# A macaron decoder layer on one core: the gate-and-up sevens read a bank on VectorE and store from GpSimd, and loads, norms and an SSD merge are re-timed

## The chip, the cores and the metric

The kernel runs on one core of a Trainium2 chip. It is written by hand against the engines: TensorE (PE) multiplies, VectorE (DVE), ScalarE (ACT) and GpSimd (POOL) do the elementwise work, SyncE (SP) issues most of the transfers, and ACT and POOL issue some. The metric is the device time of one execution in microseconds; of several executions the median is taken. The median before is 2687.21 us (three runs, 2687.17 to 2689.84).

## The reference

One decoder layer on 1024 tokens of width 1024, all in float32:

```python
f = swiglu(rmsnorm(h, ffn1_pre_g), ffn1_w_gu, ffn1_w_down)
h = h + 0.5 * rmsnorm(f, ffn1_post_g)
m = hybrid_mixer(rmsnorm(h, mix_pre_g), ...)   # stick-breaking attention | Mamba-2 SSD, then w_out
h = h + rmsnorm(m, mix_post_g)
c = memory_cross_attention(rmsnorm(h, xa_pre_g), rmsnorm(mem, mem_g), xa_wq, xa_wkv, xa_wo)
h = h + rmsnorm(c, xa_post_g)
f = swiglu(rmsnorm(h, ffn2_pre_g), ffn2_w_gu, ffn2_w_down)
h = h + 0.5 * rmsnorm(f, ffn2_post_g)
```

with `swiglu(h, w_gu, w_down) = (silu(g) * u) @ w_down`, where `g` and `u` are the halves of `h @ w_gu`, and a hidden width of 2816. `rmsnorm` divides by the root of the mean square over the width and multiplies by a gain.

## The kernel before

**Precision.** Each float32 operand is split into a high and a low part (`split`, L262: the high part is a ScalarE cast, L263, the low part a VectorE subtraction, L265). A product takes three matmuls of 128x512: high x high, low x high, high x low (`mm3`). Names that end in `hi`/`h` and `lo`/`l` are such parts; `wraw`, `raw`, `oraw` are tiles as they were loaded.

**Stages.** In the order of time: ffn1's up half (to 457 us), its down half (`down_first`, to about 640), the mixer's SSD projections and scan (`ssd`, about 740 to 1040), attention (to about 1600), the mixer's output (`mix_out`, to about 1750), cross-attention (`xattn`, to about 2040), ffn2's up half (to about 2490) and its down half.

**The sevens.** The up half of each ffn computes gate and up for pairs of feature blocks by a scheme that needs seven products for eight. One call of `seven` (L751) makes a pair `f`: seven products of twelve matmuls each into PSUM banks (`a`, `b`, `c`, `m6`), and between them VectorE, ScalarE and GpSimd add and subtract what the banks hold. There are 38 sevens, 19 in each ffn. The first product goes to `t5` and the second to `d` by ScalarE copies (L758, L762); GpSimd takes `d - t5` (L763, the name `sq` in the profile); VectorE adds the third product to make `e` (L768), and so on; L782 writes the result `t0` (`ft`), L786 and L788 are the last readers of the banks, L789 on GpSimd makes the other result `t1`. Both results are stored to DRAM (`act`) by `store`, which puts the transfer on ScalarE's queue (L622), some 4500 ns of the planner's clock later. The `ft` tiles rotate over NFT buffers, three in ffn1 and four in ffn2. The operands of the seven products are sums and differences of weight blocks, made by GpSimd (L706, `wc`) ahead of time and then split.

**The down half of ffn1** works the same way over units of `act` and `w_dn`; its weight sums (`wsum`, L946 through `add`) start while the last seven still runs.

**What sets the order.** The program order of TensorE is fixed by `_pe` (L100): each matmul is made to follow the one before, and `self.clock` adds an assumed cost of each. Work that is due at a clock time lies in `self.later` and is emitted by `run_later`; `pinned` ties a block to a clock time; `merge` (L156) interleaves two generators in proportion to two given times. For the other engines a scheduler orders the instructions by data and priority; `urgent` (L96) raises the priority. Every engine then runs its own list in order: an instruction that waits holds all behind it.

**Norms.** `post` (L395) books the steps of a post-norm: `cols` (`rms_cols`, L317: TensorE sums `acc` over partitions, `small` in the profile's name, then a root on ScalarE and a reciprocal on VectorE), `rows` (`rms_rows`, L341: a diagonal `dg` on VectorE, L347, and a product with ones), eight `apply` steps, and the columns and rows of the next pre-norm. `times` holds the clock offsets of the first three, `step` the distance of the applies, `tail` the offsets of the pre-norm's two. `sumsq` (L362) squares on ScalarE and adds on VectorE (L370), with a last addition L372 into `acc`. `flush` empties the list and takes over the next norm.

**SSD start.** `bc` (L1360 and after) makes two small products into a `seg` bank, of which there are two; VectorE's L1366 and ScalarE's L1367 empty it.

**Mixer output.** `load` (L1985) loads a piece `oraw`, squares it on ScalarE (L1979 for the first, L1982), and makes `ohi`/`olo` or `xh`/`slo` (`scaled_split`, ScalarE L270 and VectorE L272).

## Time and profile before

| | us |
|---|---|
| median of three runs | 2687.21 |
| profiled execution | 2692.84 |
| its span, first to last instruction | 2691.1 |
| before the first matmul, after the last | 6.9, 7.4 |
| mean granted TensorE clock | 0.987 |

The span is 1.7 us less than the profiled execution's own time, and that execution is 5.6 us longer than the median of the runs. In the rows of the profile a line number is that of the source before; a row names the engine, the line, the operation and output <- inputs; "[x <-y]" at its end says that the engine stood idle for x us just before and what ended that. In the windows each engine's number is its busy time, and the number in brackets the instructions that began.

### The profile page before, as it was taken

What the parts mean: (1) busy time and instruction counts of PE and PEld (TensorE: products, weight loads), DVE (VectorE), ACT (ScalarE), POOL (GpSimd) and SP (SyncE); (2) the same over time, 40 slices, a digit from 0 to 9 for tenths busy, and PEclk for the clock granted to TensorE, in tenths of its full rate; (3) what the DMA queues carried; (4) which work ended last, traced back from release to release, by engine and by line L of the source; (5) the groups of instructions that cost most, each with busy time, mean ns of one, the idle gap of its engine ahead of it and who ended that gap; (6) DMA issues with size and microseconds to landing.
All of it is one profiled execution on the core that took longest, in us unless ns stands there. A gap on an engine that the chain in (4) does not pass through costs nothing. (4 is left out here: it accounts for less than half of the span.)

```text
span 2691.1 us, 36606 instructions
## 1 busy us (share of the span) xinstructions
PE 2602.1 (97%) x12712; PEld 2149.9 (80%) x12712; DVE 1978.3 (74%) x3003; ACT 1272.9 (47%) x2317; POOL 575.7 (21%) x660
## 2 busy tenths in 40 slices
PE   8999999998999999999999999999999999999998
PEld 7788887887777778888888787778777787878887
DVE  7888886888678774777777876674447888876675
ACT  7544443545357783445444553254345443343442
POOL 1655652001100000000000001121112655553000
PEclk9999999998999999999999999999999999999999
DMA  5689887764711225434333468687567455555976
GB/s 207 236 280 316 293 287 242 250 200 152 257 66 47 71 68 188 118 96 113 110 103 107 152 200 315 223 286 248 195 221 269 161 177 193 189 191 196 353 265 219
DMA packets 229593, 528.87 MB, mean 197 GB/s; under 512 B 27936, under 2 KB 37024, under 8 KB 229408
## 3 DMA queue, kind: packets, MB, share of 16 engines
q1 hardware_dynamic: 192352, 419.56, 47.3%
q0 software_dynamic: 24384, 83.90, 8.6%
q10 hardware_dynamic: 12672, 23.07, 2.3%
q8 instruction: 100, 1.64, 0.2%
q14 instruction: 85, 0.70, 0.1%
HBM read 353.41 MB, written 152.04 MB: 188 GB/s over the span
## 5 line engine op out<-in xcount | busy, mean ns | idle before, releaser
L138 PE MATMUL mm<-xh,whi 128*128 128x512 f32 x1288 | 512.3, 407 | 11.4 <-ACT xh L270 6.9
L138 PE MATMUL mm<-xh,wlo 128*128 128x512 f32 x1240 | 479.5, 394 | 0.0
L138 PE MATMUL mm<-xl,whi 128*128 128x512 f32 (+1 forms) x1220 | 477.9, 392 | 0.9 <-DVE xl L265 0.6
L138 PEld LDWEIGHTS mm<-xh,whi 128*128 128x128 f32 x1288 | 244.2, 190 | 55.7 <-ACT xh L270 6.9
L138 PEld LDWEIGHTS mm<-xh,wlo 128*128 128x128 f32 x1240 | 234.4, 189 | 52.3 <-issue 1.3
L138 PEld LDWEIGHTS mm<-xl,whi 128*128 128x128 f32 x1220 | 231.3, 190 | 34.7 <-DVE xl L265 1.4
L1789 DVE TENSOR_TENSOR_SCAN nb<-nb,begin 128x128 f32<-128x128 f32 (+7 forms) x128 | 171.7, 1352 | 57.4 <-ACT nb L1785 56.9
L1785 ACT ACTIVATE nb<-z,scale 128x128 f32<-128x128 f32 (+2 forms) x192 | 108.0, 581 | 88.6 <-PE z L138 87.4
L1822 POOL MEMSET ath<- 128x128 f32 x64 | 13.1, 205 | 496.5 <-PE mm L138 496.5
L263 ACT CAST whi<-wraw 128x1024 fp32r<-128x1024 f32 (+1 forms) x89 | 81.1, 911 | 68.6 <-PE mm L138 37.5
L626 ACT ACTIVATE ft<-ft 128x512 f32<-128x512 f32 x88 | 55.4, 631 | 109.7 <-DVE ft L625 102.2
L706 POOL TENSOR_TENSOR wc<-wraw,raw 128x512 f32<-128x512 f32 x58 | 89.9, 1551 | 70.4 <-DVE whi L265 22.9
L138 PE MATMUL dn<-xh,wlo 128*128 128x512 f32 x296 | 102.1, 393 | 1.7 <-ACT sq L758 1.7
L706 POOL TENSOR_TENSOR wc<-raw,wraw 128x512 f32<-128x512 f32 x56 | 87.3, 1558 | 67.6 <-DVE wlo L265 20.3
L265 DVE TENSOR_TENSOR wlo<-wraw,whi 128x1024 fp32r<-128x1024 f32 x61 | 74.5, 1221 | 34.2 <-ACT whi L263 33.8
L789 POOL TENSOR_TENSOR ft<-ft,e 128x512 f32<-128x512 f32 x38 | 61.9, 1628 | 133.9 <-DVE e L788 66.8
L370 DVE TENSOR_TENSOR acc<-acc,sq 128x512 f32<-128x512 f32 x84 | 56.4, 686 | 46.3 <-ACT sq L369 42.0
L138 PE MATMUL dn<-xh,blk 128*128 128x512 f32 x280 | 90.3, 389 | 0.0
L263 ACT CAST ath<-tr 128x512 fp32r<-128x512 f32 (+1 forms) x108 | 58.9, 547 | 64.5 <-PE tr L141 62.2
L138 PE MATMUL dn<-xh,whi 128*128 128x512 f32 x256 | 88.7, 392 | 0.0
L138 PE MATMUL mm<-ath,v 128*128 128x256 f32 x320 | 85.9, 291 | 2.1 <-DVE sq L1962 2.1
L265 DVE TENSOR_TENSOR atl<-tr,ath 128x512 fp32r<-128x512 f32 (+1 forms) x108 | 67.9, 631 | 24.1 <-ACT ath L263 24.0
(558 smaller groups left out, 6775.6 us busy)
## 6 DMA issues: line engine op xcount, KB each, us to landing
whi<-dwhi SPq DMA_DIRECT2D x57, 512.0 KB, 3.4
wlo<-dwlo SPq DMA_DIRECT2D x57, 512.0 KB, 4.2
wraw<-act SPq DMA_DIRECT2D x102, 256.0 KB, 4.4
raw<-act SPq DMA_DIRECT2D x96, 256.0 KB, 4.5
wraw<-in_w_gu SPq DMA_DIRECT2D x44, 512.0 KB, 4.0
act<-ft ACTq DMA_DIRECT2D x88, 256.0 KB, 2.6
raw<-in_w_gu SPq DMA_DIRECT2D x38, 512.0 KB, 4.4
khi<-whi POOLq DMA_DIRECT2D x30, 512.0 KB, 4.6
```

Source lines behind the costliest of these rows:

```text
L138: self._pe(self.nc.tensor.matmul(out, lhsT, rhs, start=start, stop=stop, skip_group_check=self.more), cost)
L263: self.kp(self.nc.scalar.copy(hi, src))
L265: (eng or self.nc.vector).tensor_tensor(out=lo, in0=src, in1=hi.bitcast(F32), op=ALU.subtract)
L370: self.kp(nc.vector.tensor_tensor(out=accs[i % 2], in0=accs[i % 2], in1=sq, op=ALU.add))
L626: nc.scalar.activation(t, t, AF.Silu)
L706: nc.gpsimd.tensor_tensor(out=t, in0=a, in1=b, op=op)
L789: nc.gpsimd.tensor_tensor(out=t1, in0=t1, in1=e, op=ALU.mult)
L1785: nc.scalar.activation(nb[:, s0:s1], z[:, 0:n], AF.Sigmoid, scale=sc[:, i : i + 1])
L1789: nc.vector.tensor_tensor_scan(out=nb[:, 0:Wd][:, ::-1], data0=nb[:, 0:Wd][:, ::-1], data1=begin[:, S - Wd : S][:, ::-1], initial=0.0, op0 ...
L1822: nc.gpsimd.memset(x[:, 0, :].bitcast(F32), 0.0)
```

## The change

It has nine parts.

1. In `seven`, the second product is no longer copied to SBUF by ScalarE and reduced by GpSimd: VectorE subtracts `t5` from the bank into `d` (new L770).
2. `t1` is stored by a GpSimd transfer right after GpSimd's product that makes it (new L798), instead of by ScalarE later.
3. In ffn2's first block (`f == PLAIN and not begin`), three of the seven sums are made by GpSimd before the first `yield`, into tiles `ts` and `tc` (new L708).
4. In `down_first`, the weight sums of all units but the first two are ordered behind the last reader of the last seven's bank (`self.emptied`).
5. In `down_first`, the squares are urgent, and the clock offsets of both post-norms change.
6. `bc`'s two readers are urgent, and the two given times of the merge at the SSD start change from 3800 against 12110 to 4330 against 9072.
7. `oraw` gets eight buffers instead of four.
8. The mixer's post-norms get `tail` offsets of their own, (18000, 0) and (22000, 0) instead of the default; in `xattn` the steps booked up to `self.posted` are emitted at s == 2, and the rest is flushed at s == 3 instead of 2.
9. Cross-attention's post-norm gets times (8000, 15500, 18500) instead of (7000, 12000, 15000).

```diff
@@ -457,6 +457,7 @@
             c2 = self.t(self.rp, [P, 4], F32, f"cpre{hh}", bufs=2)
             r2_ = self.t(self.rp, [P, H], F32, f"rpre{hh}", bufs=1) if spread else None
             t1, t2 = tail or (t1 + 4000, t2 + 4000)
+            self.posted = T0 + t + 900
             q.append((t + t1, lambda: self.rms_cols([accs2], c2)))
             if spread:
                 q.append((t + t2, lambda: self.rms_rows(c2[:, :], r2_)))
@@ -695,12 +696,19 @@
         def pieces(f):
 
             G, U = (load(wgu[2 * f + i], [P, KT, P]) for i in range(2))
-            yield
             G0, G1, U0, U1 = G[:, 0:4], G[:, 4:8], U[:, 0:4], U[:, 4:8]
-            for a, b, op in (
+            work = [
                 (G0, G1, ALU.add), (U1, None, None), (G0, U1, ALU.add), (U0, G0, ALU.subtract), (G0, None, None),
                 (G1, U1, ALU.subtract), (U0, U1, ALU.add),
-            ):
+            ]
+            if f == PLAIN and not begin:
+                for n, tag, bufs in ((0, "ts", 1), (2, "tc", 2), (3, "tc", 2)):
+                    a, b, op = work[n]
+                    t = self.t(sp2, [P, 4, P], F32, tag, bufs=bufs)
+                    nc.gpsimd.tensor_tensor(out=t, in0=a, in1=b, op=op)
+                    work[n] = t, None, None
+            yield
+            for a, b, op in work:
                 if b is not None:
                     t = self.t(sp, [P, 4, P], F32, "wc", bufs=NWC)
                     nc.gpsimd.tensor_tensor(out=t, in0=a, in1=b, op=op)
@@ -759,8 +767,7 @@
             b = bank()
             product(b, B21)
             with self.urgent():
-                nc.scalar.copy(d, b)
-            nc.gpsimd.tensor_tensor(out=d, in0=d, in1=t5, op=ALU.subtract)
+                nc.vector.tensor_tensor(out=d, in0=b, in1=t5, op=ALU.subtract)
             c = bank()
             product(c, S[1])
             e = es.pop() if es else self.t(sp, [P, H], F32, "e")
@@ -785,10 +792,10 @@
             with self.urgent():
                 nc.vector.tensor_tensor(out=t0, in0=t0, in1=b, op=ALU.mult)
             with self.urgent():
-                nc.vector.tensor_tensor(out=e, in0=e, in1=b, op=ALU.subtract)
+                self.emptied = nc.vector.tensor_tensor(out=e, in0=e, in1=b, op=ALU.subtract).ins
             nc.gpsimd.tensor_tensor(out=t1, in0=t1, in1=e, op=ALU.mult)
             store(f, 0, t0)
-            store(f, 1, t1)
+            nc.gpsimd.dma_start(out=act_d[f // 2][1][:, f % 2, :], in_=t1)
 
         self.nblk = -1
         Wb = blocks()
@@ -943,7 +950,7 @@
             return x[:, 0], x[:, 1]
 
         def add(o, x, y, op):
-            nc.vector.tensor_tensor(out=o, in0=x, in1=y, op=op)
+            return nc.vector.tensor_tensor(out=o, in0=x, in1=y, op=op)
 
         def taker(operands, ahead):
             order = [(p, b) for p in (1, 5, 2, 6, 3, 7, 4) for b in range(NFF // 2)]
@@ -997,7 +1004,9 @@
                 nc.sync.dma_start(out=d, in_=w(0, 1))
                 o = parts(tile, x), parts(place(), y)
                 t = wsum[b] = held(spots[b])
-                add(t, d, y, ALU.subtract)
+                i = add(t, d, y, ALU.subtract)
+                if b > 1:
+                    self._after(i.ins, self.emptied)
                 return o
             if p == 5:
                 x, y = load(a(1, 0), a(1, 1))
@@ -1050,8 +1059,9 @@
         accs = [self.new_accs(), None]
 
         def squares(hh, dh, i0):
-            for i in four:
-                self.sumsq(accs[hh], i0 + i, F[hh][dh][i])
+            with self.urgent():
+                for i in four:
+                    self.sumsq(accs[hh], i0 + i, F[hh][dh][i])
 
         pair = [banks(1), banks(0)]
         product(pair[0])
@@ -1078,7 +1088,7 @@
         squares(0, 1, 4)
         self.norm_pool = self.dnp, 4
         self.XH = [[self.t(self.xp, [P, H], F32R, f"xh{hh}{d}") for d in range(KT)] for hh in range(2)]
-        self.post(0, gpost, self.C[0], gnext, step=4700, accs=accs[0], times=(5000, 8500, 11000), tail=(4500, 8000))
+        self.post(0, gpost, self.C[0], gnext, step=4300, accs=accs[0], times=(8000, 11500, 13500), tail=(4200, 7700))
         ps = banks(0)
         product(ps)
         self.norm_pool = self.msp, 1
@@ -1100,7 +1110,7 @@
             update(F[1][0][i], F[1][0][i], ps[i], ALU.subtract)
             self.sumsq(accs[1], 4 + i, F[1][0][i])
         self.flush(0)
-        self.post(1, gpost, self.C[1], gnext, step=2400, accs=accs[1], times=(4000, 7500, 9500), tail=(15500, 21000))
+        self.post(1, gpost, self.C[1], gnext, step=2400, accs=accs[1], times=(4500, 9500, 11500), tail=(13500, 19000))
 
     def down_seven(self, sp, rw, wdn, act_d, sums_d, out):
 
@@ -1363,8 +1373,9 @@
                 ps = self.t(pp, [P, 2, P], F32, "seg", bufs=2)
                 self.mm(ps[:, 0, :], Bt[:, cs], Ct[:, cs], True, True)
                 self.tr(ps[:, 1, :], Bt[:, cs])
-                nc.vector.tensor_tensor(out=cbm[:, c, :], in0=ps[:, 0, :], in1=self.tri, op=ALU.mult)
-                nc.scalar.copy(Bl[:, c, :], ps[:, 1, :])
+                with self.urgent():
+                    nc.vector.tensor_tensor(out=cbm[:, c, :], in0=ps[:, 0, :], in1=self.tri, op=ALU.mult)
+                    nc.scalar.copy(Bl[:, c, :], ps[:, 1, :])
 
             def early(qd, c):
                 hs = slice(4 * qd, 4 * qd + 4)
@@ -1608,7 +1619,7 @@
 
             for _ in range(6):
                 next(fill)
-            self.merge(first(), 3800, fill_some(fill, 14), 1730 * 14 / 2)
+            self.merge(first(), 4330, fill_some(fill, 14), 648 * 14)
             self.merge(chunks(), 86500, fill, 144000)
             gates()
             self.run_all(keys(6, 8))
@@ -1983,7 +1994,7 @@
                     nc.vector.tensor_tensor(out=asum[-1], in0=asum[-1], in1=sq, op=ALU.add)
 
             def load(kt, hh):
-                raw = self.t(sp, [P, H], F32, "oraw", bufs=4)
+                raw = self.t(sp, [P, H], F32, "oraw", bufs=8)
                 nc.sync.dma_start(out=raw, in_=self.mix_d[kt][:, hh * H : (hh + 1) * H])
                 if kt < 8:
                     square(kt, raw)
@@ -2045,11 +2056,11 @@
                     R.update({i: norm_row(i, 1, 500 + 1000 * i) for i in range(2)})
                 if n == 1:
                     self.run_later(float("inf"))
-                    self.post(0, "mix_post_g", None, "xa_pre_g", step=5000, spread=False)
+                    self.post(0, "mix_post_g", None, "xa_pre_g", step=5000, spread=False, tail=(18000, 0))
                     self.resid(1, 5000, 17000)
                 if n == 3:
                     self.flush(0)
-                    self.post(1, "mix_post_g", None, "xa_pre_g", step=3000, spread=False)
+                    self.post(1, "mix_post_g", None, "xa_pre_g", step=3000, spread=False, tail=(22000, 0))
 
 
     def xattn(self):
@@ -2173,12 +2184,14 @@
                         self.run_all(out_part(ps, next(W), 0, 0, 8))
                         out_copy(ps, 0)
                     self.run_later(float("inf"))
-                    self.post(0, "xa_post_g", None, "ffn2_pre_g", step=5000)
+                    self.post(0, "xa_post_g", None, "ffn2_pre_g", step=5000, times=(8000, 15500, 18500))
                 if s + 2 < 8:
                     load(K, s + 2, "k", 2, 0)
                 if s == 6:
                     self.resid(1, 4000)
                 if s == 2:
+                    self.run_later(self.posted)
+                if s == 3:
                     self.flush(1)
                 if s < 7:
                     step = zip_(values(s), scores(s + 1))
```

How the order on the engines moves, at three places.

GpSimd, around the ends of the first two sevens in ffn1 (`wc` are weight sums, `ft<-ft,e` the product that makes `t1`, `sq<-sq,sq` the subtraction into `d`). Before:

```order
L706 TENSOR_TENSOR wc_1244<-raw_302_1023,wraw_1021 128x512
L789 TENSOR_TENSOR ft_1053<-ft_1053,e_181 128x512
L706 TENSOR_TENSOR wc_1292<-wraw_1021,raw_302_1023 128x512
L763 TENSOR_TENSOR sq_311_1099<-sq_311_1099,sq_310_1098 128x512
L706 TENSOR_TENSOR wc_1322<-raw_302_1023 128x512
L706 TENSOR_TENSOR wc_1350<-raw_328_1173 128x512
L706 TENSOR_TENSOR wc_1399<-raw_328_1173,wraw_1175 128x512
L706 TENSOR_TENSOR wc_1428<-wraw_1175,raw_328_1173 128x512
L789 TENSOR_TENSOR ft_1211<-ft_1211,e_1165 128x512
L706 TENSOR_TENSOR wc_1476<-raw_328_1173,wraw_1175 128x512
L763 TENSOR_TENSOR sq_347_1273<-sq_347_1273,sq_346_1272 128x512
```

The same place in the change, where line numbers above 700 are 7 to 13 higher:

```order
L714 TENSOR_TENSOR wc_1242<-raw_302_1022,wraw_1020 128x512
L796 TENSOR_TENSOR ft_1052<-ft_1052,e_181 128x512
L798 DMA act_45_155<-ft_1052 128x512
L714 TENSOR_TENSOR wc_1291<-wraw_1020,raw_302_1022 128x512
L714 TENSOR_TENSOR wc_1319<-raw_302_1022 128x512
L714 TENSOR_TENSOR wc_1347<-raw_328_1171 128x512
L714 TENSOR_TENSOR wc_1396<-raw_328_1171,wraw_1173 128x512
L714 TENSOR_TENSOR wc_1425<-wraw_1173,raw_328_1171 128x512
L796 TENSOR_TENSOR ft_1209<-ft_1209,e_1163 128x512
L798 DMA act_47_157<-ft_1209 128x512
L714 TENSOR_TENSOR wc_1474<-raw_328_1171,wraw_1173 128x512
```

The subtraction is gone from each seven, and a transfer of the result stands behind each product that makes one.

TensorE, at the start of the SSD scan (`seg<-Ct,Bt` with the row behind it is one pair into a `seg` bank; `mm<-xh..` are matmuls of the projection that is merged in). Before:

```order
L138 MATMUL mm_7144<-xl_1317_6087,whi_7047 128x512
L138 MATMUL mm_7144<-xh_1244_5801,wlo_7048 128x512
L138 MATMUL seg_7167<-Ct_6840,Bt_6839 128x128
L141 MATMUL seg_7167<-ident_112,Bt_6839 128x128
L138 MATMUL seg_7172<-Ct_6840,Bt_6839 128x128
L141 MATMUL seg_7172<-ident_112,Bt_6839 128x128
L138 MATMUL seg_7177<-Ct_6840,Bt_6839 128x128
L141 MATMUL seg_7177<-ident_112,Bt_6839 128x128
L138 MATMUL seg_7182<-Ct_6840,Bt_6839 128x128
L141 MATMUL seg_7182<-ident_112,Bt_6839 128x128
L138 MATMUL seg_7187<-Ct_6840,Bt_6839 128x128
L141 MATMUL seg_7187<-ident_112,Bt_6839 128x128
```

In the change:

```order
L138 MATMUL seg_7111<-Ct_6821,Bt_6820 128x128
L141 MATMUL seg_7111<-ident_112,Bt_6820 128x128
L138 MATMUL mm_7080<-xh_1255_5793,whi_6996 128x512
L138 MATMUL mm_7080<-xl_1444_6671,whi_6996 128x512
L138 MATMUL mm_7080<-xh_1255_5793,wlo_6997 128x512
L138 MATMUL seg_7119<-Ct_6821,Bt_6820 128x128
L141 MATMUL seg_7119<-ident_112,Bt_6820 128x128
L138 MATMUL mm_7080<-xh_1256_5794,whi_6996 128x512
L138 MATMUL mm_7080<-xl_1447_6693,whi_6996 128x512
L138 MATMUL mm_7080<-xh_1256_5794,wlo_6997 128x512
L138 MATMUL seg_7127<-Ct_6821,Bt_6820 128x128
L141 MATMUL seg_7127<-ident_112,Bt_6820 128x128
```

The last five of the eight pairs stood one behind the other; now three projection matmuls stand between every two pairs.

ScalarE, at the start of the mixer's output (`ohi` and `xh` are high parts of the loaded pieces, `sq` their squares, `whi` the high parts of two weight tiles). Before:

```order
L270 ACTIVATE ohi_15755<-oraw_15750,params_78 128x512
L263 CAST whi_15889<-wraw_15887 128x1024
L1982 ACTIVATE sq_3322_15752<-oraw_15750 128x512
L270 ACTIVATE ohi_15764<-oraw_15759,params_78 128x512
L270 ACTIVATE ohi_15773<-oraw_15768,params_78 128x512
L1982 ACTIVATE sq_3326_15761<-oraw_15759 128x512
L270 ACTIVATE ohi_15782<-oraw_15777,params_78 128x512
L263 CAST whi_15899<-wraw_15897 128x1024
L1982 ACTIVATE sq_3330_15770<-oraw_15768 128x512
L270 ACTIVATE ohi_15791<-oraw_15786,params_78 128x512
```

In the change:

```order
L270 ACTIVATE ohi_15736<-oraw_15731,params_78 128x512
L270 ACTIVATE ohi_15745<-oraw_15740,params_78 128x512
L1993 ACTIVATE sq_3322_15733<-oraw_15731 128x512
L270 ACTIVATE ohi_15754<-oraw_15749,params_78 128x512
L270 ACTIVATE ohi_15763<-oraw_15758,params_78 128x512
L270 ACTIVATE ohi_15772<-oraw_15767,params_78 128x512
L1993 ACTIVATE sq_3326_15742<-oraw_15740 128x512
L263 CAST whi_15870<-wraw_15868 128x1024
L263 CAST whi_15880<-wraw_15878 128x1024
L1993 ACTIVATE sq_3330_15751<-oraw_15749 128x512
```

The first weight cast stood behind the fourth high part and now stands behind all eight; the second, which stood behind the seventh, follows it at once.

## The prediction

> **What bounds the kernel now.** I read the busy shares first, then the waits of TensorE, then the granted clock around those waits, and then the engines' own rows at each of them.
>
> ```profile
> span 2691.1 us, 36606 instructions
> PE 2602.1 (97%) x12712; PEld 2149.9 (80%) x12712; DVE 1978.3 (74%) x3003; ACT 1272.9 (47%) x2317; POOL 575.7 (21%) x660
> ```
>
> TensorE is the bound: it is busy for 2602.1 of 2691.1 us. No matmul is added or taken away, so at most the idle 89 us and what hangs on them can be won. The table of TensorE's waits says where they are (total, times, longest):
>
> ```profile
> PE dn L138 <- DVE acc L372: 8.9, 1, 8.9
> PE dn L138 <- DVE e L768: 8.8, 6, 4.9
> PE ms L138 <- DVE acc L372: 7.1, 2, 4.6
> PE ms L138 <- DVE dg L347: 5.8, 3, 3.0
> PE mm L138 <- DVE e L768: 3.9, 3, 2.5
> PE dn L138 <- DVE wlo L265: 3.7, 4, 2.7
> PE seg L138 <- ACT Bl L1367: 2.9, 2, 1.6
> PE dn L138 <- DVE e L788: 2.2, 1, 2.2
> PE dn L138 <- ACT whi L263: 2.1, 2, 1.6
> PE mm L138 <- ACT whi L263: 1.9, 1, 1.9
> PE mm L138 <- DVE whi L265: 1.7, 1, 1.7
> PE dn L138 <- ACT sq L758: 1.7, 1, 1.7
> ```
>
> These are few and short, and they sit in the places that the diff touches; they add up to 50.7 us. But a wait costs more than itself. Windows over two of them (us, PE busy and starts, the other engines, granted clock, DMA):
>
> ```profile
> 611.40:620.30 8.90, 0.01 (x1) 0.00 (x0) 8.19 (x15) 5.84 (x10) 0.00 (x0) 0.61 0.39 126
> 620.30:627.03 6.73, 6.70 (x20) 5.64 (x21) 5.16 (x12) 1.39 (x3) 0.00 (x0) 0.50 0.25 78
> 627.03:649.00 21.97, 21.97 (x97) 17.80 (x96) 20.12 (x32) 14.76 (x26) 3.24 (x6) 1.00 0.49 156
> 1736.30:1739.80 3.50, 3.50 (x10) 2.71 (x9) 1.08 (x2) 0.00 (x0) 0.00 (x0) 0.51 0.18 47
> ```
>
> At full clock a matmul starts every 0.227 us (97 in 21.97). The last row follows the wait of 2.6 us at 1734 (ms, L372): there the clock is halved for 3.4 us, in which a matmul takes 0.43 and up: about 3.4/2 = 1.6 to 1.7 us more. After the wait of 8.9 us it is halved for twice as long (620 to 627). So I price a wait of about 2 us and more at its own length plus 1.6 us for each halved stretch of 3.4 us, and one that stands alone below about 1.7 us at its own length.
>
> [...]
>
> **The change part by part.** Gains are for the whole place, wait and slow clock together; in brackets the bounds.
>
> *The sevens.* The second product's copy on ScalarE and GpSimd's subtraction become one subtraction on VectorE that reads the bank.
>
> ```profile
> L762 ACT COPY sq<-dn x22: 580/590/593, 114.4 to 2451.0; 128x512 f32<-128x512 f32 x22
> L763 POOL TENSOR_TENSOR sq<-sq,sq x38: 1287/1736/1763, 96.2 to 2451.8; 128x512 f32<-128x512 f32 x38
> 94.37 0.68 DVE L265 TENSOR_TENSOR xl<-bh,xh 128x512 fp32r<-128x512 f32 x1
> 98.33 1.75 DVE L265 TENSOR_TENSOR whi<-wc,whi 128x512 fp32r<-128x512 f32 x1
> 100.00 0.68 DVE L768 TENSOR_TENSOR e<-sq,dn 128x512 f32<-128x512 f32 x1
> 100.73 1.22 PE L138 MATMUL dn<-S,wlo 128*128 128x512 f32 x2 [4.88 <-DVE e L768]
> 200.00:219.05 19.05, 19.05 (x86) 15.78 (x85) 16.59 (x21) 9.73 (x18) 11.07 (x8) 1.00 0.95 320
> ```
>
> Per seven, ScalarE loses 0.59 us, GpSimd 1.74 less the 0.54 of issuing its new store (its row stands below, at the rivals), and VectorE gains 0.68: L768 at 100.00 is the nearest row, since it too reads one bank. VectorE has room for it (16.59 busy of the 19.05 that a seven takes). It also gets some back: a split takes 0.68 us alone (94.37), but 1.75 while GpSimd works (98.33), whereas VectorE's rows with a bank stay at 0.68. The difference d is ready 0.68 us after the product instead of 0.59 + 1.74, so e comes 1.5 us earlier, more where splits stood in between. First seven of ffn1: working the rows forward from product b, e ends near 98.6 instead of 100.68, so a wait of 2.75 stays of 4.88: 3.3 us [0, 7.5]. The other waits for e, all in ffn2 and all but one about a microsecond and less, come to 3.9 + 1.4 us by the table, with a slow first matmul (0.50 for 0.39) behind each of the seven: all go, 6.0 [3, 7.5].
>
> ```profile
> 2118.99 0.59 ACT L758 COPY sq<-dn 128x512 f32<-128x512 f32 x1 [4.47 <-POOL ft L789]
> 2125.12 4.15 PE L138 MATMUL mm<-S,whi 128*128 128x512 f32 x10 [2.48 <-DVE e L768]
> ```
>
> In the first row ScalarE stood 4.47 us behind its own store, which waited for GpSimd's product; TensorE's waits of 1.7 (sq, L758) and 2.48 followed, and a halved window. Both causes go: 5.8 by the price, 5.5 [3, 6.3]. At the first seven of ffn2 (mm <- whi, 1.9 and 1.7) the hoisted sums are ready before their splits ask for them; with two halved windows 6.8, of which I take 5.5 [2, 7], since the third block's sum may still be late.
>
> *End of ffn1's up half.* The weight sums now wait for the last bank read.
>
> ```profile
> 452.15 0.69 DVE L946 TENSOR_TENSOR xh<-xl,raw 128x512 f32<-128x512 f32 x1 [1.82 <-DMA raw<-in_w_dn]
> 453.50 0.96 PE L138 MATMUL dn<-whi,wlo 128*128 128x512 f32 x3 [1.06 <-DVE ft L782]
> 456.69 3.53 PE L138 MATMUL dn<-whi,wlo 128*128 128x512 f32 x8 [2.23 <-DVE e L788]
> ```
>
> VectorE stood 1.82 us for a load with the bank's readers behind it. 1.06 + 2.23 + 1.6 = 4.9; I take 4.8 [2, 5.3]. The sums come later, but their first readers are some units away.
>
> *Norms.* At 620.33 TensorE's row moves behind 14 more matmuls (3.2 us), and VectorE's order up to the sum that it waits for is the same as before. So 5.7 of 8.9 us stay. What comes after is VectorE's: 20.12 of 21.97 us busy in the windows above. TensorE, earlier by 3.2, meets the same VectorE at the next norm (677.84, L347, 3.0 us). The two places hold 18 us, and I book 2 [-3, 10]. The mixer's post-norm columns (2.57 and 4.56 us, L372) move behind 32 and 60 more rows of TensorE, over 7 us, more than either wait: 4.2 [2, 4.4] and 6.5 [3, 7]. Cross-attention's rows (1926.65, 2.45 us, L347) move 16 rows, 3.6 us: 4.2 [1, 4.7].
>
> *SSD.*
>
> ```profile
> 785.27 0.80 PE L138 MATMUL seg<-Ct,Bt 128*128 128x128 f32 x2 [1.60 <-ACT Bl L1367]
> ```
>
> Five pairs in a row wait for two banks. With three matmuls (0.68 us) between pairs and urgent readers the rows give one wait of about 0.9 us, at the third pair: VectorE's products cannot start before the tile that they write is free. 2.9 - 0.9 = 2.0, and of the two halved windows behind them (3.2) I take 2, because the state update's wait soon after hangs on ScalarE's exponents, which come no earlier: 4.0 [1.5, 6].
>
> *Mixer loads.* Eight instead of four load buffers. ScalarE now makes all eight parts before the two weight casts.
>
> ```profile
> 1611.15 1.22 DVE L265 TENSOR_TENSOR wlo<-wraw,whi 128x1024 fp32r<-128x1024 f32 x1
> 1612.42 0.50 PE L138 MATMUL dn<-ohi,wlo 128*128 128x512 f32 x1 [2.68 <-DVE wlo L265]
> 1637.59 0.63 ACT L1979 ACTIVATE asum<-oraw 128x512 f32<-128x512 f32 x1 [0.96 <-DMA oraw<-mix]
> 1639.21 0.50 PE L138 MATMUL dn<-ohi,whi 128*128 128x512 f32 x1 [1.62 <-ACT whi L263]
> ```
>
> The low half at 1611.15 gets an eighth residual (0.65 us) ahead of it on VectorE, so the wait before 1612.42 grows by 0.6; the scale row near 1626, whose diagonal now stands behind another weight split, may cost 0.4 more: -1 [-5, 2]. The wait at 1639.21 came from loads late in four buffers; it goes with 0.53 behind it and its halved window: 4 [1, 4.3].
>
> **Sum:** sevens 3.3 + 6.0 + 5.5 + 5.5 = 20.3, end of up 4.8, norms 2 + 4.2 + 6.5 + 4.2 = 16.9, SSD 4.0, mixer 3.0: 49.0 us. The profiled execution took 2692.84, so 2643.8; it lies 5.6 above the median 2687.21, so 2638.2, said 2638.
>
> **Rivals.**
> (a) *Handed on.* Half of the gains come back as waits a few us later, as I work out for 620/678. For it: VectorE's 20.12 of 21.97. Against: in the sevens it has 2.5 us spare. 49/2: 2662.5.
> (b) *All of it goes,* the norm of ffn1 too: 49 + 16 + 4 (the halves of bracketed terms) = 69: 2618. For it: VectorE still has 2.3 of the 15.6 us from 611.4 to 627 free. Against: nothing on VectorE's way to that norm is shorter.
> (c) *Only waits are won, the slow windows stay,* because some idle remains at each place. Nine are booked: one each near 457, 1640, 1736, 1927, 2125, two each near 785 and 2085: 49 - 9 x 1.6 = 34.6: 2652.6. [...]
> (d) *Slower: the store's queue.* A seven's `ft` buffer is free only when GpSimd's store has landed. The rows of GpSimd's product (its first at 110.8, in the first seven), of the buffer's next writer (124.7, in the second), of loads issued on GpSimd and of the stores as they are:
>
> ```profile
> L789 POOL TENSOR_TENSOR ft<-ft,e x38: 1272/1638/1765, 110.8 to 2466.1; 128x512 f32<-128x512 f32 x38
> L782 DVE TENSOR_TENSOR ft<-sq,mm x16: 674/676/689, 124.7 to 2443.4; 128x512 f32<-128x512 f32 x16
> L391 POOL DMA_DIRECT2D xl<-h x48: 536/538/582, 1616.0 to 2481.6; - x48
> DMA to landing us min/median/max: 2.9/7.4/10.5
> act<-ft ACTq DMA_DIRECT2D x88, 256.0 KB, 2.6
> ```
>
> The store leaves at 110.8 + 1.6 = 112.4; from a landing of 12 us on it stalls VectorE, with the bank readers behind it. At 14 us the 19 sevens of ffn1, with the smaller pool, pay 2 + 1.6 each, 68 us: 2687 - 49 + 68 = 2706. For it: the queue also carries the blocks' loads. Against: the longest landing, 10.5, leaves 1.8 us, the median nearly 5. [...]
> (e) *Nothing:* every wait returns in full elsewhere, or the reordered rows cost what they win: 2687. For it: the place at 1612. Against: most waits have no busy engine behind them.
>
> **Chances.** Forecast 0.54, (a) 0.20, (b) 0.11, (c) 0.04, (d) 0.07, (e) 0.04. About 0.2% (5.4 us) is what the measurement can tell from no change. Faster: 0.54 + 0.20 + 0.11 + 0.04 - 0.01 for the weakest of (a) = 0.88; same 0.05; slower 0.07. The brackets of the terms alone add up to 2615 and 2677 if all fell on one side, which they won't; taking in (b) and (a) I say 2617 to 2666.
>
> **What would show it.** Right: no L768 among TensorE's waits in ffn2; one wait under 3.5 us near 98; none near 454, 784, 1640, 1734, 1816, 1926; 5 to 6 us left near 617 and again a wait at the row norm near 675; 2.5 to 3.5 near 1612; a granted clock of 0.99. Wrong: waits for `ft` or for GpSimd's store; L770 late on VectorE with the first product's copy waiting; at 617 a wait under 3 us (then (b)); new waits near 1622 to 1627.

## The result, and the profile after

The changed kernel takes 2641.71 us (median of four runs, 2639.28 to 2644.32) where the kernel before takes 2687.19: a ratio of 0.9829, 95% interval 0.9812 to 0.9846, some 45 us. The forecast was 2638, with a range of 2617 to 2666. The profiled execution took 2642.43 us. Below are the span and the busy times (first part of the page) of the changed kernel.

```profile
span 2640.5 us, 36639 instructions
PE 2580.4 (98%) x12712; PEld 2138.5 (81%) x12712; DVE 1972.0 (75%) x3041; ACT 1263.3 (48%) x2281; POOL 530.1 (20%) x660
```

TensorE's 12712 matmuls are the same and their busy time fell by 21.7 us, because fewer of them run at half clock (13 halved stretches before, 5 after, start and end of the program aside); its idle time fell by 29. GpSimd lost 45.6 us of work. VectorE got 38 more instructions and is busy 6.3 us less: it pays for its new work in time that it no longer loses beside GpSimd, as the first experiment shows. Its new line reads a bank and never takes longer than a plain one (0.69 us at most, against 0.68 for a split alone; by line and operation; minimum, median and maximum ns):

```profile
L770 DVE TENSOR_TENSOR sq<-dn,sq x22: 676/683/692, 113.1 to 2402.4; 128x512 f32<-128x512 f32 x22
L770 DVE TENSOR_TENSOR sq<-mm,sq x16: 677/686/692, 93.2 to 2386.2; 128x512 f32<-128x512 f32 x16
```

TensorE's waits in the changed kernel (total us, times, longest), those that answer to the rows quoted in the prediction:

```profile
PE dn L138 <- DVE acc L372: 5.3, 1, 5.3
PE ms L138 <- DVE dg L347: 4.7, 5, 2.2
PE dn L138 <- DVE e L775: 4.4, 2, 2.7
PE mm L138 <- DVE e L775: 3.0, 1, 3.0
PE ms L138 <- DVE acc L372: 2.5, 1, 2.5
PE dn L138 <- ACT whi L263: 1.5, 1, 1.5
PE dn L138 <- DVE wlo L265: 1.5, 1, 1.5
```

Ten waits for e (15.0 us) became three (7.4). The rows for L788, whi in ffn2, sq L758 and the mixer's columns (7.1, acc) are gone. Two of the three waits that stayed are in ffn2 (2.96 at 2084 and 1.64 at 2105), where the prediction's signs of being right had none. Where the larger ones that stayed lie, in TensorE's own rows:

```profile
98.04 2.50 PE L138 MATMUL dn<-S,wlo 128*128 128x512 f32 x5 [2.74 <-DVE e L775]
612.57 1.87 PE L138 MATMUL dn<-small,acc 128*128 128x1 f32 x8 [5.27 <-DVE acc L372]
660.83 1.05 PE L138 MATMUL ms<-small,acc 128*128 128x1 f32 x8 [2.54 <-DVE acc L372]
1594.88 0.50 PE L138 MATMUL dn<-ohi,whi 128*128 128x512 f32 x1 [1.53 <-ACT whi L263]
1597.14 0.50 PE L138 MATMUL dn<-ohi,wlo 128*128 128x512 f32 x1 [1.52 <-DVE wlo L265]
1612.39 1.10 PE L138 MATMUL ms<-dg,onesr 128*128 128x512 f32 x2 [2.22 <-DVE dg L347]
2084.51 3.06 PE L138 MATMUL mm<-S,whi 128*128 128x512 f32 x12 [2.96 <-DVE e L775]
```

To compare place by place I took, in both traces, each interval from one matmul's start to the next less the median interval of its kind: the time lost to waits and slow clock together. It adds up to 158.4 us before and 109.0 after, 49.4 less; the prediction's sum was 49.0.

| place (time before) | before | after | won | booked |
|---|---|---|---|---|
| first seven of ffn1 (100) | 8.5 | 6.8 | 1.7 | 3.3 |
| end of ffn1's up half (453 to 457) | 5.3 | 0 | 5.3 | 4.8 |
| the two norms (620, 678) | 18.0 | 14.7 | 3.3 | 2 |
| SSD start (785) | 12.0 | 9.0 | 3.0 | 4.0 |
| mixer's output (1612, 1639) | 9.3 | 6.5 | 2.8 | 3.0 |
| mixer's post-norm columns (1734, 1816) | 11.6 | 0 | 11.6 | 10.7 |
| cross-attention's rows and after (1926 to 2053) | 11.5 | 9.1 | 2.4 | 4.2 |
| first seven of ffn2 (2085) | 7.0 | 1.7 | 5.2 | 5.5 |
| second seven of ffn2 (2119 to 2125) | 6.3 | 3.2 | 3.1 | 5.5 |
| later waits for e in ffn2 | 8.0 | 1.9 | 6.1 | 6.0 |
| end of ffn2's up half | 2.3 | 0.7 | 1.6 | 0 |

Some 3 us more went in places that the change does not touch; how such scatter comes about is the subject of the last section.

### The profile page after: what moved, and what is told of

Same layout as the page of the kernel before. It is cut to its first block, busy times and chain, and to the rows that moved or that the text cites. A ratio compares the mean times of both kernels' runs of the same rounds, so it can differ in the third digit from the quotient of the medians.

```text
span 2640.5 us, 36639 instructions
## 1 busy us (share of the span) xinstructions
PE 2580.4 (98%) x12712; PEld 2138.5 (81%) x12712; DVE 1972.0 (75%) x3041; ACT 1263.3 (48%) x2281; POOL 530.1 (20%) x660
## 3 DMA queue, kind: packets, MB, share of 16 engines
q8 instruction: 100, 1.64, 0.3%
## 4 chain that ended last, share of the span: by engine, by line
PE 79%; DVE 9%; DMA 5%; ACT 3%; issue 2%; POOL 0%; SPq 0%; DVEq 0%; ACTq 0%
PE mm L138 45%; PE dn L138 24%; PE z L138 2%; PE ms L138 2%; PE tr L141 2%; PE y L138 1%; DMA wraw<-act 1%; PE ms L141 1%; DMA raw<-in_w_dn 1%; DVE hl L265 1%; DMA raw<-act 1%; DVE wlo L265 1%; PE seg L138 1%; DVE F L953 1%; DVE whi L265 1%
```

## The experiments

The theory is the prediction's: each part takes away one cause at its own place, and with it the slow clock behind. The main rivals are that a gain is handed on to a later wait, and that a part does nothing of its own. So first each part was undone by itself. In every short diff - is the changed kernel and + the experiment. "Over the changed kernel" is the difference of the two ratios to the kernel before (0.9829 and the experiment's), times 2687. Each ratio's interval reaches some 4 us to either side (7 for part 6), so that a difference of less than about 6 us is not shown by the times alone; there the place in the trace has to show it. A line number is that of the kernel's own source.

**The subtraction back on ScalarE and GpSimd (part 1).**

```diff
-                nc.vector.tensor_tensor(out=d, in0=b, in1=t5, op=ALU.subtract)
+                nc.scalar.copy(d, b)
+            nc.gpsimd.tensor_tensor(out=d, in0=d, in1=t5, op=ALU.subtract)
```

> The changed kernel with part 1 alone undone (ScalarE copies the second product again and GpSimd subtracts; the store stays on GpSimd). Theory: the subtraction stood in e's way, so the short waits for e in ffn2 (8.0 us with their slow restarts before) and 1.7 of the wait near 98 us come back: 2649 to 2651, with six or more waits for e among TensorE's. Rival: e was late because VectorE's own list was late (as at 2084 us of the changed kernel, where a wait of 2.96 us for e is left): 2641 to 2643.

2658.36 us, ratio 0.9896 (0.9881 to 0.9911): 18 over the changed kernel by the ratios and 14 by the time lost in the trace, about twice what the theory expected; the rival expected none. The waits for e are now eleven, 18.2 us, one of them longer than any in ffn2 before. TensorE's waits, and VectorE's rows at the longest one in ffn2, of this experiment:

```profile
PE dn L138 <- DVE e L776: 11.1, 7, 4.9
PE mm L138 <- DVE e L776: 7.1, 4, 4.7
```

```profile
2079.87 4.71 DVE L265 TENSOR_TENSOR blk<-wraw,blk 128x512 fp32r<-128x512 f32 x1
2084.51 0.68 DVE L889 TENSOR_TENSOR dg<-dg,xl 128x512 f32<-128x512 f32 x1
2085.11 0.67 DVE L776 TENSOR_TENSOR e<-sq,mm 128x512 f32<-128x512 f32 x1
```

GpSimd's rows there:

```profile
2080.31 2.50 POOL L714 TENSOR_TENSOR wc<-raw 128x512 f32<-128x512 f32 x2
2082.77 1.26 POOL L771 TENSOR_TENSOR sq<-sq,sq 128x512 f32<-128x512 f32 x1
```

A split that takes 0.68 alone took 4.71 here, beside two of GpSimd's sums and the subtraction. So the subtraction costs in two ways. In two of the ten longest waits (1.40 and 1.32 us) d itself comes last, and in a third (0.75) together with the bank. In the seven others, the two longest among them, d was there 0.5 to 2.1 us before e began, and what ended last was VectorE's own list, as the rival had it, with splits that are slow beside GpSimd; here d was ready at 2084.03 and e began at 2085.11. In the two up halves 115 splits took more than 0.75 us in the kernel before, 75 in the changed kernel and 114 here. VectorE is busy for 1991.7 us in this kernel, 19.7 more than with the 38 subtractions of its own. Splits, with both inputs in SBUF, went from 0.68 us alone to 4.71 beside GpSimd here, and to 2.94 in the changed kernel; there L770, with one input in a bank, stays within 0.692 in all 38. Why the two differ is not shown.

**The store back on ScalarE (part 2).**

```diff
-            nc.gpsimd.dma_start(out=act_d[f // 2][1][:, f % 2, :], in_=t1)
+            store(f, 1, t1)
```

> The changed kernel with part 2 alone undone (t1 is stored by ScalarE's queue again). Theory: ScalarE stands behind its store again; the wait of 1.7 us for the first product's copy in ffn2 comes back with part of a halved window, and 1 to 2 us at ffn2's up to down: 2644 to 2647. Rival one: without GpSimd's subtraction t1 is made early enough for the store not to block: 2641 to 2643. Rival two: the transfers on GpSimd's queue held up its sums, so undoing is a gain: 2636 to 2639.

2643.11 us, ratio 0.9837 (0.9822 to 0.9852): not to be told from 0.9829, the time that rival one gave, but not for its reason. ScalarE does stand behind its store again: 31 times, 82.0 us in all, the longest 3.8, waiting for GpSimd's product before its next copy (30 times and 77.7 us in the kernel before, the longest 4.5). It has that time to spare: TensorE has no wait for this copy, where the kernel before had one of 1.7. The move does no harm either, which settles rival (d) of the prediction; the issues of the changed kernel's store on GpSimd (duration, then from issue to landing):

```profile
L798 POOL DMA_DIRECT2D act<-ft x38: 580/586/593, 111.8 to 2419.4; - x38
DMA to landing us min/median/max: 2.3/2.6/5.8
```

The longest landing, 5.8 us, is less than half of the 12 from which, by the prediction's estimate, it would have stalled.

**Four load buffers again (part 7).**

```diff
-                raw = self.t(sp, [P, H], F32, "oraw", bufs=8)
+                raw = self.t(sp, [P, H], F32, "oraw", bufs=4)
```

> The changed kernel with four load buffers in the mixer's output instead of eight. Theory: the wait before 1639 us of the kernel before comes back (4.3 us with its halved window), the places near 1595 and 1612 go from 6.5 back to about 5: 2643 to 2646. Rival: the buffers only move the waits and the sum over this stage stays: 2641 to 2643.

2649.15 us, ratio 0.9863 (0.9847 to 0.9880): 9 over the changed kernel, more than the 1 to 4 expected; in its trace the mixer's output loses 7 to 8 us more. One late load holds ScalarE (first row) and with it the copy of a scale row, and TensorE waits (second):

```profile
1643.29 0.72 ACT L270 ACTIVATE ohi<-oraw,params 128x512 fp32r<-128x512 f32 x1 [7.08 <-DMA oraw<-mix]
```

```profile
1647.32 1.39 PE L138 MATMUL ms<-dg,onesr 128*128 128x512 f32 x2 [3.71 <-ACT rn L356]
```

**The three hoisted sums back in their place (part 3)**, one edit: the block under `if f == PLAIN and not begin` in `pieces` is left out.

> The changed kernel with part 3 alone undone (no sums ahead in ffn2's first block). Theory: the two waits for whi at the start of ffn2's sevens come back (3.6 us, 7.0 with the halved windows): 2645 to 2649. Rival: they were late because of GpSimd's other work, which is less now: 2641 to 2643.

2648.05 us, ratio 0.9855 (0.9840 to 0.9870): 7 over. Both waits of before return, with two halved windows; the place loses 6.6 us (booked 5.5):

```profile
2050.98 0.50 PE L138 MATMUL mm<-xh,whi 128*128 128x512 f32 x1 [1.80 <-ACT whi L263]
2053.41 1.22 PE L138 MATMUL mm<-xh,whi 128*128 128x512 f32 x2 [1.69 <-DVE whi L265]
```

**The weight sums not held back (part 4).**

```diff
-                if b > 1:
-                    self._after(i.ins, self.emptied)
```

> The changed kernel with the weight sums of ffn1's down half no longer ordered behind the last bank reader of the last seven (part 4 undone). Theory: VectorE again stands about 1.8 us for a load with the bank's readers behind it, and TensorE loses 5 us near 453 to 457 (5.27 before, 0 after): 2646 to 2648 us where the changed kernel takes 2641 to 2643. Rival: the gain there came from the other parts (the difference read from the bank ends the last seven earlier), then the place stays empty without part 4 and the time stays 2641 to 2643.

2647.49 us, ratio 0.9847 (0.9827 to 0.9866): 5 over, which the time alone does not show; the place shows it, as the theory said. VectorE stands 1.76 us for a load again (448.86, L953), and TensorE waits for the bank behind it; the place loses 4.6:

```profile
450.21 0.96 PE L138 MATMUL dn<-whi,wlo 128*128 128x512 f32 x3 [0.21 <-DVE ft L789]
453.39 5.30 PE L138 MATMUL dn<-whi,wlo 128*128 128x512 f32 x15 [2.23 <-DVE e L795]
```

**The mixer's and cross-attention's norm steps at their old times (parts 8 and 9)**: the two `tail` offsets, `times` and the early `run_later(self.posted)` are left out, and the flush is at s == 2.

> The changed kernel with the mixer's and cross-attention's post-norm steps at their offsets of before (parts 8 and 9 undone). Theory: each of these waits stands alone, with no busy engine behind it, so nothing of the gain was handed on: waits return near 1734 (4.4), 1816 (7.2) and 1926 (4.7), less what cross-attention now has at 1926 to 1933 (2.7): 12 to 16 us, 2654 to 2658. Rival (handed on): moved columns and rows only made later waits in cross-attention and ffn2, half of it comes back: 2648 to 2650.

2656.80 us, ratio 0.9883 (0.9864 to 0.9902): 14.5 over. The three waits are back to the hundredth, with their slow windows (6.0, 7.2 and 4.9 us):

```profile
1713.43 1.72 PE L138 MATMUL ms<-small,acc 128*128 128x1 f32 x8 [2.57 <-DVE acc L372]
1797.11 1.84 PE L138 MATMUL ms<-small,acc 128*128 128x1 f32 x8 [4.56 <-DVE acc L372]
1907.22 1.16 PE L138 MATMUL ms<-dg,onesr 128*128 128x512 f32 x2 [2.45 <-DVE dg L347]
```

The mixer's two waits were handed on to nowhere, as the theory said. Cross-attention's row loses 4.9 us here and 1.2 in the changed kernel. The stretch behind it, up to ffn2, loses 8.3 here, 7.9 in the changed kernel and 6.6 in the kernel before: the 1.3 that came back there is lost without these two parts too, so it was not handed on by them. Which part it hangs on was not tried.

**The SSD start as before (part 6)**: the two readers not urgent, and the merge at 3800 against 12110.

> The changed kernel with the SSD start's readers not urgent and its merge at the times of before (part 6 undone). Theory: the waits for the seg banks return, 3 to 4 us (the place near 785 to 800 lost 11.97 before and 8.97 after): 2645 to 2646. Rival: what is won there is lost at the state update behind it, which hangs on ScalarE's exponents: 2641 to 2643.

2647.96 us, ratio 0.9857 with a wide interval (0.9831 to 0.9883): 7 over, where 3 to 4 were expected and 3.4 stand at the place itself (two waits of 1.34 and 1.60 for Bl instead of 0.81 and 0.19). The rest is at places that this edit does not touch.

**ffn1's norms at their old times, squares not urgent (part 5).**

```diff
-        self.post(0, gpost, self.C[0], gnext, step=4300, accs=accs[0], times=(8000, 11500, 13500), tail=(4200, 7700))
+        self.post(0, gpost, self.C[0], gnext, step=4700, accs=accs[0], times=(5000, 8500, 11000), tail=(4500, 8000))
```

> The changed kernel with the squares of ffn1's down half not urgent and both its post-norms' offsets as before (part 5 undone). Theory: one wait of about 8.9 us near 617 and one of 3 near 678 return in place of 5.3 and 2.5, and the slow stretches with them: the two places lose 18 again instead of 14.7, so 2644 to 2646. Rival: VectorE's load there sets the end of both norms whatever their offsets, then 2641 to 2643, with the loss shifted between the two places.

2644.81 us, ratio 0.9841 (0.9823 to 0.9858): 3 over, at the edge of what can be told. The two waits are 9.23 and 2.83 again, and the two places lose 17.3 instead of 14.8 (15.7 in a second profile of the changed kernel): the amount moves between the places, and little of it goes, as the prediction had it. Whether the part is worth anything is not shown.

The costs of the parts, undone one at a time, add up to 66 us by the ratios and 59 by the traces, where the whole change won 45 and 49. So they are not independent terms of a sum; some of the surplus is scatter at places that an edit does not touch, and the mixer's loads cost more undone (7 to 8 us at their place) than they won (2.8).

**The changed kernel once more, and VectorE's order mended.** The one step of the sum that clearly failed is the second seven of ffn2. The prediction said of the wait for e there that its cause goes with GpSimd's subtraction. VectorE's rows at that place, in the kernel before (first two rows) and in the changed kernel, say otherwise:

```profile
2122.73 1.74 DVE L881 TENSOR_TENSOR dg<-dg,xl 128x512 f32<-128x512 f32 x1
2124.39 0.68 DVE L768 TENSOR_TENSOR e<-sq,mm 128x512 f32<-128x512 f32 x1
```

```profile
2076.35 3.48 DVE L265 TENSOR_TENSOR blk<-wc,blk 128x512 fp32r<-128x512 f32 x2
2079.75 0.68 DVE L770 TENSOR_TENSOR sq<-dn,sq 128x512 f32<-128x512 f32 x1
2080.35 2.90 DVE L265 TENSOR_TENSOR blk<-wraw,blk 128x512 fp32r<-128x512 f32 x1
2083.18 0.68 DVE L888 TENSOR_TENSOR dg<-dg,xl 128x512 f32<-128x512 f32 x1
2083.78 0.67 DVE L775 TENSOR_TENSOR e<-sq,mm 128x512 f32<-128x512 f32 x1
```

In the kernel before, d was ready at 2123.92, and a weight sum (L881) held e for 0.5 us more. In the changed kernel d is ready at 2080.43, but ahead of the two bank reads (L770, L775) stand three splits of coming blocks, the last slowed to 2.90 beside two of GpSimd's sums, and a weight sum (L888). They are not urgent; why the scheduler put them there is not shown. The new theory: the order of VectorE's list is the cause. The rival: VectorE is short of time there, and the splits would be late instead. In the experiment a split stands, in the first three sevens, behind the newest of these bank reads (`front`) that the program has written by then:

```diff
-                self.split(w[:, 0], w[:, 1], a)
+                i = self.split(w[:, 0], w[:, 1], a)
+                if self.front is not None:
+                    self._after(i, self.front)
...
-            self.later += [(T0 + 94000 + 28000 * b + t, f) for t, f in chain(b)]
+            self.later += [(T0 + 112000 + 28000 * b + t, f) for t, f in chain(b)]
...
-                    R[2] = norm_row(2, 0, 13000)
+                    R[2] = norm_row(2, 0, 16000)
```

> The changed kernel once more, unaltered, beside the next one on the same chip. It also tests a reading of the clock: TensorE's clock seems to be halved, window by window of 3.41 us from a start that differs from run to run, after each window in which TensorE idled about half or more. Theory: the same waits stand at the same places, but a wait of 1.5 to 3.4 us costs a halved window in one run and none in another, by where it lies (2084, 1595, 1612, 1015); time 2639 to 2648. Rival: the clock follows the wait's length alone, then the same waits are followed by the same slow stretches as in the first profile of this kernel.

> The changed kernel with VectorE's list re-ordered by hand at the waits that stayed: in the first three sevens of each ffn the splits of coming blocks stand behind the last read of a bank that the program has written by then; ffn2's weight sums start 18 us later; the mixer's scale row near 1612 moves 13 matmuls later. Theory (the waits for e that stayed are VectorE's own order, splits and weight sums ahead of bank reads): the waits at 2084 and 2105 and the row's at 1612 go, the one at 98 shrinks by 1 to 2: 6 to 9 us less than the unaltered changed kernel beside it, 2632 to 2639. Rival (VectorE is simply short of time there, slowed beside GpSimd): the splits are late instead, TensorE waits for whi, wlo or blk near 2080 to 2100, and no more than the 2 to 4 us of the row at 1612 are won.

On one chip: 2643.86 us unaltered (ratio 0.9830, 0.9816 to 0.9843) and 2640.16 re-ordered (0.9818, 0.9805 to 0.9831): less than expected, and not to be told apart. The unaltered kernel already differs from its first profile: its waits at 1612 (2.22) and 2105 (1.64) are not there, and that at 2084 is 3.84 instead of 2.96, so the expectation that the same waits stand failed in part. Place by place the theory holds where both have a wait: at 98 the wait is 0.47 instead of 2.74, and of the 7.4 us that the place lost in the unaltered kernel 2.2 are left; the wait at 2084 is gone; no split is late. For 1612 and 2105 this pair shows nothing. What was won was lost again at two places that the edit made itself, both with a halved window:

```profile
2118.20 2.24 PE L138 MATMUL mm<-S,blk 128*128 128x512 f32 x7 [1.96 <-DVE e L779]
2430.59 5.79 PE L138 MATMUL dn<-whi,hl 128*128 128x512 f32 x12 [2.55 <-ACT whi L263]
```

The first is the fourth seven, to which no order was given and in which the later weight sums now fell; at the second, ScalarE stood 8.51 and 1.31 us for loads of the down half, beside which the last weight sums, 18 us later, now ran; that these were the cause is supported only by the next run, where they end earlier and the wait is gone. Both were mended: the order in six sevens and for the weight sums too, these at 106000 + 26500 b, and in the mixer's output two of the eight parts behind the first weight block's split, against the two waits of 1.5 at 1595 to 1597.

> The re-ordered kernel of the run before, mended where its profile showed new waits: the order of VectorE's list is fixed in the first six sevens of each ffn and for ffn2's weight sums too; these begin 12 us later than in the changed kernel but end 3 us earlier; in the mixer's output two parts' splits stand behind the first weight block's split, on ScalarE and VectorE. Theory: the waits at 98 (2.7 to 3.4, with halved windows), 2084 and 1612 stay away, those at 2118 (2.0) and 2430 (2.6) of the run before go, the two at 1594 to 1597 (1.5 each) shrink to under 1: 9 to 13 us less than the changed kernel, 2630 to 2635. Rival: VectorE has no room in ffn2's first sevens, the waits only move to the next list: 2638 to 2642.

2634.96 us, ratio 0.9791 (0.9777 to 0.9806), 10 us less than the changed kernel by the two ratios and 55 less than the kernel before (2689.69 on this chip): the fastest of all. At 98 and 1612 nothing is left to speak of, at 2084, 2118 and 2430 nothing; at 1595 one wait of 1.94 with a halved window stands instead of two of 1.5, where under 1 was expected. Three waits for e (1.27, 2.24, 0.79) came in later sevens, without a halved window. By the time lost in the traces the kernel wins 7 us (101.5 against 108.7): 10 at 98, 2084 and 2105, of which those three take 5 back, so some of it may have moved on, as the rival had it.

**One thing more: the norm at 612.** In the changed kernel VectorE stands for late loads (1.45, 0.78 and 0.47 us from 599 to 604) with the four bank sums of the post-norm behind it. Here the operands of the sixth product are made later and put behind these sums (`summed`):

```diff
+                pin = self.summed[1 if b == 1 else 3] if b else None
+                if pin is not None:
+                    self._after(i.ins, pin)
```

> The kernel beside it with one thing more, in ffn1's down half: the operands of the sixth product are made one unit ahead instead of five until the bank sums before the post-norm (L953) are written, and those of its second unit and after stand behind these sums on VectorE, whose list until now stood about 5 us for late loads with the sums behind it. Theory: the post-norm's column sum comes 2 to 4 us earlier, and the 8.8 us at 612 shrink to 3 to 5; the wait at 661 stays or grows by 1, since VectorE is full until 655: 2 to 5 us less than the kernel beside it. Rival: the sixth product's second unit is late instead (TensorE waits 1 to 3 us for hl near 601 to 604) and nothing or less than nothing is won.

2638.32 us, ratio 0.9806 (0.9792 to 0.9820), 3 to 4 more than its neighbour: neither theory nor rival. The column sum indeed comes 9 us earlier on VectorE (its last addition, L375, at 599.04; in the kernel beside it at 607.95), TensorE's wait for it is gone, and the second unit is late by 0.59 only. But the next step now waits:

```profile
600.99 2.14 PE L138 MATMUL mm<-hl,wlo 128*128 128x512 f32 x8 [0.59 <-DVE hl L265]
616.98 2.08 PE L138 MATMUL dn<-dg,onesr 128*128 128x512 f32 x2 [8.17 <-DVE dg L350]
```

```profile
611.68 0.16 DVE L335 TENSOR_TENSOR cpost<-dn,cpre 128x4 f32<-128x4 f32 x1
614.90 0.17 DVE L340 RECIPROCAL cpost<-cpost 128x4 f32<-128x4 f32 x1
616.25 0.68 DVE L350 TENSOR_TENSOR dg<-ident,cpost 128x512 f32<-128x512 f32 x1
```

From column to diagonal the norm has five small steps on VectorE, and between each two of them the list holds splits of later units. That is handing on in its plainest form. Whether the row, moved some 8 us later or its steps made urgent, would keep the gain was not tried.

## Why the prediction was right, and where it was not

Against the profiled execution, on which the sum was made, the forecast was 2643.8 and 2642.43 came. The median came out 3.5 above its forecast, because the profile of before lay 5.6 over its median and that of after only 0.7; this correction was the less certain step. That the sum itself (49.0 against 49.4) fits to half a microsecond is in part luck: six places of the table won less than booked, 7.3 us together, five won 4.4 more, and 3.3 came from places that nobody touched.

- *The price of a wait* (its length and 1.6 us for each halved stretch) held for the sum, and rival (c), only the waits won, is out: at 1734, 1816, 454 and 2085 the slow windows went with the waits, and of 13 halved stretches 5 are left. It did not hold place by place, as the last section shows.
- *First seven of ffn1:* the wait that was to stay of 2.75 stayed as 2.74. The term of 3.3 was sized too high because the halved stretch stayed whole (97.96 to 104.79 before, 96.38 to 103.20 after): 1.7.
- *Second seven of ffn2, "Both causes go":* this step failed for the second cause. The first, the store, went: ScalarE no longer stands, and the wait for sq is gone. The wait for e did not: it is 2.96 (3.84 in the second profile) where it was 2.48, and the place won 3.1 where 5.5 were booked. Its cause is VectorE's list, as the re-ordered kernels show: d is now ready 3.35 us before e begins, and with the splits ordered behind the bank reads and the weight sums later (both changed at once) the wait is gone.
- *Part 1 as a whole* was booked at 3.3 + 6.0 and a share of the 5.5; undone beside all the other parts it costs 18 (14 by the trace). The step that was too small is the one that let VectorE "get some back": beside GpSimd its splits lost more than the row of 1.75 showed (up to 4.71), and VectorE's busy time fell by 19.7.
- *Norms:* 5.7 were to stay at 620 and 5.27 did (6.3 in the second profile), and at the next norm a wait of 2.54 on its columns stands where 3.0 stood on its rows; together 3.3 won (2.3 by the second profile) where 2 were booked. The last experiment shows how the wait moves on to the next step when the column sum comes earlier still.
- *Mixer's and cross-attention's steps:* 4.2 and 6.5 came as 4.4 and 7.2; the second was booked with one halved window, and two stood there (1814.87 to 1821.69). Of the 4.2 at 1926 the row gave 3.7, and 1.3 went again in the stretch behind it, but not through these parts: it is lost there with them undone too. So rival (a) is not shown at this place.
- *Mixer loads:* the loss of 1 at 1612 came out as about 1.5 in one profile and 2.2 in the other. The scale row, booked at 0.4, waits 2.22 in the first and not at all in the second; the two waits ahead of it (1.53 and 1.52, in the second 1.87 and 1.52) meet a halved clock in the second alone. Undone, the part costs 9, more than its terms: four buffers also delay the second half's scale row.
- *Small slips:* 0.59 + 1.74 - 0.68 is 1.65, not 1.5 us, and 1.62 + 0.53 + 1.6 is 3.75, booked as 4; the table of waits leaves out rows of places that the change does not touch, the longest 6.9 us (xh, L270).
- *Rival (d)* had landings of 12 us and more as its point of decision; the longest is 5.8.

## What to carry to other kernels

Moving GpSimd's subtraction to VectorE made VectorE's busy time smaller here (1991.7 to 1972.0 us), since its reads of a bank cost the same beside GpSimd (0.69 at most) and its splits do not (0.68 alone, up to 4.71). Before a wait is put down to the operation that feeds it, read the list of the engine that it names: what stands there ahead of it may be work that nobody needs yet, and giving that order by hand was worth 7 us by the traces and 10 by the times. A wait that hangs on a chain of small steps moved along the chain here when its first link got earlier (8.17 us at the diagonal instead of 6.33 at the column), so look at all links; that moving all of them keeps the gain was not tried.

## What the hardware showed that was not expected

In these traces the halved stretches of TensorE's clock lie on a grid with a step of 3.413 us. In the profile of the changed kernel the halved stretches begin at 96.38, 611.79, 662.99, 779.04 and 1017.97 us: 151, 15, 34 and 70 times 3.413 us apart. The first two last 6.83 us, the others 3.41. In the second profile of the same kernel two of them begin at 1595.92 and 2084.03, 143 times 3.413 us apart, but 439.3 and 582.3 times from 96.38: the same step from another start. A window is one step of this grid here. Stretches over three places in the two profiles show what went with it (us, PE busy and starts, other engines, granted clock, DMA share, GB/s); first the changed kernel, then the same again:

```profile
1016.76:1018.05 1.29, 1.29 (x10) 1.29 (x11) 0.85 (x2) 0.29 (x1) 0.00 (x0) 0.97 1.02 400
1018.05:1021.40 3.35, 3.35 (x18) 3.35 (x17) 0.31 (x1) 0.73 (x2) 0.00 (x0) 0.50 0.58 232
1598.30:1602.50 4.20, 4.20 (x21) 3.45 (x20) 3.14 (x6) 2.85 (x5) 1.62 (x3) 1.00 0.97 336
2084.50:2088.00 3.50, 3.49 (x15) 2.88 (x16) 2.33 (x4) 2.14 (x5) 1.68 (x1) 1.00 0.59 215
```

```profile
1016.80:1021.40 4.60, 4.60 (x38) 4.60 (x39) 1.17 (x3) 1.02 (x3) 0.06 (x1) 1.00 0.82 307
1595.90:1602.70 6.80, 6.05 (x14) 4.78 (x15) 5.55 (x8) 4.74 (x8) 2.36 (x5) 0.50 0.96 333
2083.82:2087.45 3.63, 3.63 (x9) 2.85 (x10) 2.47 (x4) 2.18 (x4) 1.67 (x1) 0.53 0.63 210
```

At 1016.8 both profiles have the same wait of 1.93 us, for the same square on VectorE. In the first it lies within one window (1014.56 to 1017.97), and the next one runs at 0.50; in the second an edge of the grid, at 1015.65, cuts it into some 0.8 and 1.1 us, and the clock stays at 1.00. At 1595 and 2084 it is the other way round: 1.48 + 1.58 and 1.39 + 1.58 us on the two sides of an edge cost no slow window in the first profile; in the second the waits are longer (3.39 and 3.84 us in all), 2.66 and 3.22 of them lie in one window, and a halved window follows (two of them at 1595). In the traces of the kernel before and of the first profile of the changed kernel, from 20 to 2600 us, all 12 windows at full clock with 1.9 us or more of idle time were followed by a halved one; of 15 with 1.4 to 1.9 us five were, of 16 with 1.0 to 1.4 us one (1.25 us, from 659.58 in the changed kernel), and of those with less none. Of the windows that were halved themselves, all 8 with 0.7 us or more of idle time were followed by another halved one, and one of the 19 with less. Two slow windows go with the wait of 2.74 us before 98.04, in the first profile: there are 1.69 us of idle time in the window before 96.38 and 1.66 in the one behind it.

```profile
96.38:99.79 3.41, 1.75 (x4) 1.46 (x5) 3.27 (x4) 1.76 (x3) 2.78 (x3) 0.50 0.00 0
99.79:103.20 3.41, 3.41 (x9) 2.64 (x9) 3.41 (x5) 1.07 (x2) 2.30 (x2) 0.50 0.01 2
```

So the waits at these places had no fixed price: the 2.96 us at 2084 cost their length alone, the 1.93 at 1016.8 their length alone or one halved window besides, the 2.74 at 98 two, each some 1.7 us more (half of 3.41), by where the grid lay. This is one source of the scatter at places that nobody had touched; the other is the waits themselves, which differ between two profiles of one kernel (2.96 and 3.84 at 2084, 2.22 and none at 1612).
